# Gate and up in three PSUM banks a set, with sets that overlap by three products

## The chip, the cores and the metric

One NeuronCore of a Trainium2 chip runs the whole program. TensorE (PE) multiplies, ScalarE (ACT), VectorE (DVE) and GpSimd (POOL) work elementwise, and SyncE (SP) issues every transfer that matters here. The metric is the device time of one execution in microseconds; lower is better. Instructions of one engine run in the order of its queue, and a wait for a semaphore holds up all that stands behind it in that queue.

## The reference

The reference is one layer of a hybrid decoder block over 2064 positions (16 meta tokens and 2048 of the sequence) with 1024 channels. What matters here is its end, the SwiGLU feed-forward net with 2816 hidden channels:

```python
        h = h + mixed @ w_out[i].astype(jnp.float32)
        n2 = rmsnorm(h, norm2_g[i])
        ff = jax.nn.silu(n2 @ w_gate[i].astype(jnp.float32)) * (n2 @ w_up[i].astype(jnp.float32))
        h = h + ff @ w_down[i].astype(jnp.float32)
```

Ahead of it stand a normalisation, one projection into a state-space group and a pooling group, their normalised sum and the projection `w_out`; behind it a last normalisation. All is float32.

## The kernel before

**Arithmetic.** A float32 product is made of three fp32r matmuls (`mm3`, lines 116 to 119): each operand is split into a high part (a cast on ScalarE, line 110) and a low part (a subtraction, line 85), and the product of the two low parts is dropped. Gate, up and down use the seven products of Strassen and Winograd in place of eight. With weight quarters a11, a12, a21, a22 and their combinations s1 to s4, and activation quarters b11, b12, b21, b22 and their combinations t1 to t4, the products of one set are a11·b11, a12·b21, s2·t2, s3·t3, s1·t1, a22·t4 and s4·b22, named below by their activation (b11, b21, t2, t3, t1, t4, b22). One product is four steps of K with three matmuls of 128x512 each, so 12 matmuls into one PSUM bank. Its results are sums: c00 = b11 + b21, c01 = b11 + t2 + t1 + b22, c11 = b11 + t2 + t3 + t1, c10 = b11 + t2 + t3 + t4.

**Stages.** Until about 581 us the program does the norms, projections, the state space part, pooling and `w_out`. From 581 to 1439 us it does gate and up: for each of two halves `b` of the sequence and each of 11 steps `f0` (two blocks of 128 hidden channels) one set for gate and one for up, which is a pair of 14 products. Then it does down until the end.

**A pair.** `wset` loads the two raw weight blocks (`load_raw`, tag "raw", four buffers) and POOL makes s1, s2, s3, s4. `part` splits each of the seven into `wch` and `wcl` (ten buffers). `seven` is a generator: it gives its seven products a PSUM bank each (`mm_tile`, four banks in all). ScalarE copies the first out to a tile `u`, and VectorE does the other sums from PSUM into `u` and into the pair's tiles `gt` and `ut` (one tag, three buffers of 8 KB a partition). Gate takes Silu of its four results in place; up multiplies its four into `gt`. Then POOL makes four combinations of the four results for the down stage, and SP stores `gt` and `ut` to `ff_d` (lines 1021 and 1022). The next set begins when the one before has issued its products.

**The activations.** The seven split activation tiles `X[...]` of one half lie in SBUF, with one buffer each. `x_rows` makes them for one row block: load, norm, transposes on PE (`ptx`), copies on ScalarE, four combinations on POOL, and for all that aren't split at once a store to `xr_d`. `x_stage(b, i, n)` loads n of them for each of four row blocks (tile `xp`, tag "raw" too, so these loads, the weight loads and the row blocks `hr` share four buffers) and splits them. For the first half t2, t3 and t4 come that way, right ahead of the first pair; x_rows of the second half runs after the pairs f0 = 2, 6, 10 and 14 of the first, and its seven x_stage tiles are loaded between the halves, under a raised priority, while the last pair of the first half runs (its weights are fetched ahead: `wg`, `wu`).

**What sets the order.** The program is written once, and a scheduler assigns each instruction a place in its engine's queue, by the order of the code, priorities and an estimate of when its inputs are there. Semaphores enforce what depends on what, the reuse of buffers and banks too.

Of the kernel before, what the change touches and what calls it, by code (L numbers as in the profile page):

```python
# [9 lines left out]
F32 = mybir.dt.float32  # L10
# [3 lines left out]
AF = mybir.ActivationFunctionType  # L14
ALU = mybir.AluOpType

P = 128
# [20 lines left out]
def kernel(  # L38
# [9 lines left out]
    V, A, GP, PE, SY = nc.vector, nc.scalar, nc.gpsimd, nc.tensor, nc.sync  # L48
    M_, A_, S_ = ALU.mult, ALU.add, ALU.subtract
# [10 lines left out]
    ff_d = [dram.tile([P, NF // 2, 7, 512], F32, name=f"ff_d{b}") for b in range(NB)]  # L60
# [23 lines left out]
    def tt(o, a, b, op, e=V):  # L84
        e.tensor_tensor(o, a, b, op=op)  # L85
# [21 lines left out]
    def split(hi, lo, src, scale=None, e=V):  # L107

        if scale is None:
            A.copy(hi, src)  # L110
            tt(lo, src, hi.bitcast(F32), S_, e)
        else:
            A.activation(hi, src, AF.Copy, scale=scale)
            stt(lo, src, scale, hi.bitcast(F32), M_, S_)

    def mm3(o, lh, ll, rh, rl, first, last):
        PE.matmul(o, lh, rh, start=first, stop=False)  # L117
        PE.matmul(o, lh, rl, start=False, stop=False)  # L118
        PE.matmul(o, ll, rh, start=False, stop=last)  # L119


    ident = const.tile([P, P], F32, name="ident")
# [163 lines left out]
    for a, b in ((0, KD), (KD, nv)):  # L286
# [3 lines left out]
        if a == 0:  # L290
# [3 lines left out]
                              then=lambda: load_slice(2))  # L294
# [335 lines left out]
    done = []  # L630
# [101 lines left out]
    for u in range(NU):  # L732
        j = T + 1 + u
# [139 lines left out]
    L0, L1 = slice(0, 512), slice(512, 1024)  # L873
    HALF = T // 2

    XN = ("b11", "b21", "t2", "t3", "t1", "t4", "b22")

    def combos(b11, b12, b21, b22, put):

# [24 lines left out]
    def w_rows(m):  # L904

        ra, rb = [xa_p.tile([P, D], F32, name="wr", tag="raw", bufs=4) for _ in range(2)]
        for j, r in enumerate((ra, rb)):
            SY.dma_start(r, w_down[0][(2 * m + j) * P:(2 * m + j + 1) * P, :])
        combos(ra[:, L0], ra[:, L1], rb[:, L0], rb[:, L1], lambda nm, row: None)
        for j, r in enumerate((ra, rb)):  # L910
            SY.dma_start(wd_d[:, m, 2 * j:2 * j + 2].rearrange("p a c -> p (a c)"), r)

    def x_stage(b, i, n):

        for nm in XN[i:i + n]:
            x_tile(xb_p if nm in ("t2", "t3", "t4") else xa_p, nm)
        for t in range(HALF):
            xp = xa_p.tile([P, D], F32, name="xp", tag="raw", bufs=4)
            SY.dma_start(xp[:, :n * 512], xr_d[b][t][:, i:i + n].rearrange("p a c -> p (a c)"))
            for q in range(n):  # L920
                put_x(XN[i + q], t, xp[:, q * 512:(q + 1) * 512], GP if b and t % 2 else V)

# [14 lines left out]
    wc_p = gu.enter_context(tc.tile_pool(name="wc", bufs=1, side="right"))  # L937
    xb_p = gu.enter_context(tc.tile_pool(name="xb", bufs=1, side="right"))

    def load_raw(w, f):  # L940
        raw = xa_p.tile([P, KD, P], F32, name="raw", tag="raw", bufs=4)
        SY.dma_start(raw, w[0][:, f * P:(f + 1) * P].rearrange("(k p) f -> p k f", p=P))
# [19 lines left out]
    def seven(ws, c, done, early=False):  # L962

        a11, a12, s2, s3, s1, a22, s4 = ws

        def prod(a, xn):
            o = mm_tile("pr")
            ah, al = a if isinstance(a, tuple) else part(a)
            for k in range(4):
                mm3(o, ah[:, k], al[:, k], X[xn][0][:, k], X[xn][1][:, k], k == 0, k == 3)  # L970
            return o

        u = wc_p.tile([P, 512], F32, name="u", tag="u", bufs=2)
        A.copy(u, prod(a11, "b11"))
        yield
        tt(c(0, 0), prod(a12, "b21"), u, A_)
        done(0, 0)
        yield
        if early:
            p5, p4 = prod(s1, "t1"), prod(s4, "b22")  # L980
        tt(u, prod(s2, "t2"), u, A_)
        yield
        tt(c(1, 0), prod(s3, "t3"), u, A_)
        yield
        if not early:
            p5 = prod(s1, "t1")
        tt(c(1, 1), p5, c(1, 0), A_)
        done(1, 1)
        tt(c(0, 1), p5, u, A_)
        yield  # L990
        tt(c(1, 0), prod(a22, "t4"), c(1, 0), A_)
        done(1, 0)
        yield
        tt(c(0, 1), p4 if early else prod(s4, "b22"), c(0, 1), A_)
        done(0, 1)
        yield

    def parts(ws):
        return [part(a) for a in ws]

    def gate_up(b, f0, wg=None, wu=None):

        gt = wc_p.tile([P, 2, 2, 512], F32, name="gt", tag="gt", bufs=3)
        ut = wc_p.tile([P, 2, 2, 512], F32, name="ut", tag="gt", bufs=3)
        gate = seven(wg or wset(w_gate, f0), lambda i, j: gt[:, i, j],
                     lambda i, j: A.activation(gt[:, i, j], gt[:, i, j], AF.Silu), b == 0 and f0 == 0)  # L1006
        if wu is None:
            for _ in gate:
                pass
        next(gate, None)  # L1010
        for _ in seven(wu or wset(w_up, f0), lambda i, j: ut[:, i, j],
                       lambda i, j: tt(gt[:, i, j], gt[:, i, j], ut[:, i, j], M_)):
            next(gate, None)
        a11, a21, a12, a22 = [gt[:, i, j] for i in range(2) for j in range(2)]
        s1, s2, s4 = ut[:, 0, 0], ut[:, 0, 1], ut[:, 1, 0]
        tt(s1, a21, a22, A_, GP)
        tt(s2, s1, a11, S_, GP)
        tt(a21, a11, a21, S_, GP)
        tt(s4, a12, s2, S_, GP)
        fl = "p i j c -> p (i j) c"  # L1020
        SY.dma_start(ff_d[b][:, f0 // 2, :4], gt.rearrange(fl))
        SY.dma_start(ff_d[b][:, f0 // 2, 4:], ut.rearrange(fl)[:, :3])

    wg, wu = wset(w_gate, 0), None
    x_stage(0, 2, 2)
    x_stage(0, 5, 1)
    for b in range(NB):
        for f0 in range(0, NF, 2):
            if b == 0 and f0 == NF - 2:
                wg = parts(wset(w_gate, f0))  # L1030
                wu = wset(w_up, f0)
            gate_up(b, f0, wg, wu)
            wg = wu = None
            if b == 0 and f0 % 4 == 2 and f0 // 4 < HALF:
                x_rows(1, f0 // 4)
            if b == 1:
                w_rows(f0 // 2)
        if b == 0:
            with tc.high_priority(offset=200):
                x_stage(1, 0, 2)  # L1040
                wg = wset(w_gate, 0)
                x_stage(1, 2, 2)
                x_stage(1, 4, 2)
                x_stage(1, 6, 1)


    NM = NF // 2
# [147 lines left out]
    for g, (i, n) in enumerate(seq):  # L1195
        if g == 0:
            o, o1 = mm_tile("pd"), mm_tile("pd")
# [5 lines left out]
        elif g == 1:  # L1203
            o = o1
        else:
            o = mm_tile("pd")
# [48 lines left out]
```

## Time and profile before

| what | value |
|---|---|
| time, median of 3 runs | 1866.21 us (1865.23 to 1866.81) |
| the profiled execution's own time | 1867.75 us |
| its span, first to last instruction | 1866.0 us |
| mean granted TensorE clock | 0.987 |
| PE busy | 1803.0 us, 97% |
| DVE, POOL, ACT busy | 1240.0, 815.2, 672.6 us |

The profile is of one execution, so what is summed from it stands against 1867.75 us, and the median of the runs lies 1.5 us lower. Busy shares are of the whole span. In a timeline each row has the start in us, the duration in us, the engine, the code line, the operation with its output and inputs, and in brackets how long the engine had been idle before it and who released it; matmuls overlap in their pipeline, so the distance from start to start is the pace, not the duration. In a table of windows each row has the window, its length, for each engine the busy time and the number of instructions, then the granted clock (PEclk), the DMA engines' share and the traffic.

### The profile page before, as it was taken

How to read it: one execution, taken by the hardware profiler on the slowest of the kernel's cores; microseconds unless marked ns; L12 is line 12 of the kernel's file. 1: busy time of each engine (PE TensorE's matmuls, PEld its weight loads, DVE VectorE, ACT ScalarE, POOL GpSimd, SP SyncE). 2: the span in 40 equal slices, each digit the busy share in tenths (PEclk: the TensorE clock that was granted, in tenths of full speed). 3: DMA queues.
4: the chain of work that ended last, by engine and by line, in shares of the span. 5: the costliest groups of instructions: out<-in, count | busy, mean ns of one | idle time of the engine just before them, and what ended most of it. 6: DMA issues, size and time to landing. Idle time of an engine off the chain costs nothing.

```text
span 1866.0 us, 23676 instructions
## 1 busy us (share of the span) xinstructions
PE 1803.0 (97%) x8497; PEld 1498.3 (80%) x8497; DVE 1240.0 (66%) x1913; ACT 672.6 (36%) x1213; POOL 815.2 (44%) x619
## 2 busy tenths in 40 slices
PE   7989997899999999999999999999999999999998
PEld 5767786788877788888887788888888888888886
DVE  6995877866456877666668877777677344446773
ACT  4332334243454433333335333333333343333431
POOL 1773425733244654654646876666562000003400
PEclk9999998999999999999999999999999999999999
DMA  6254424544255353444426664455447765537871
GB/s 184 71 178 164 159 96 156 175 170 141 94 176 166 108 163 108 159 158 129 159 97 195 210 204 133 154 178 175 140 149 234 216 206 180 156 102 213 252 220 70
DMA packets 260518, 298.37 MB, mean 160 GB/s; under 512 B 17148, under 2 KB 204048, under 8 KB 255536
## 3 DMA queue, kind: packets, MB, share of 16 engines
q1 hardware_dynamic: 260304, 296.84, 50.2%
q8 instruction: 67, 1.10, 0.2%
q14 instruction: 51, 0.42, 0.1%
q0 software_dynamic: 96, 0.01, 0.0%
HBM read 202.37 MB, written 96.53 MB: 160 GB/s over the span
## 4 chain that ended last, share of the span: by engine, by line
PE 71%; DVE 3%; DMA 2%; POOL 1%; issue 1%; ACT 1%; POOLq 0%; DVEq 0%; SPq 0%; ACTq 0%
PE pr L117 13%; PE pr L119 13%; PE pr L118 13%; PE pd L118 7%; PE pd L117 7%; PE pd L119 7%; PE po L117 2%; PE po L119 2%; PE po L118 2%; DVE wcl L85 1%; POOL s L85 1%; PE pgate L774 1%; DMA hr<-h_d 1%; PE ptx L865 1%; DMA raw<-in_w_gate_dram 1%
## 5 line engine op out<-in xcount | busy, mean ns | idle before, releaser
L85 DVE TENSOR_TENSOR wcl<-raw,wch 128x512 fp32r<-128x512 f32 x176 | 179.0, 1019 | 32.1 <-ACT wch L110 31.0
L110 ACT CAST wch<-raw 128x512 fp32r<-128x512 f32 x176 | 108.7, 622 | 252.9 <-PE pr L118 226.6
L85 DVE TENSOR_TENSOR fl<-fr,fh 128x512 fp32r<-128x512 f32 x168 | 117.0, 708 | 120.6 <-ACT fh L110 120.4
L110 ACT CAST fh<-fr 128x512 fp32r<-128x512 f32 x168 | 95.7, 584 | 190.2 <-PE pd L118 165.0
L110 ACT CAST wch<-s 128x512 fp32r<-128x512 f32 x132 | 82.0, 622 | 223.8 <-PE pr L118 163.8
L85 POOL TENSOR_TENSOR s<-raw 128x512 f32<-128x512 f32 x44 | 67.3, 1531 | 167.1 <-DVE wcl L85 70.2
L85 DVE TENSOR_TENSOR wcl<-s,wch 128x512 fp32r<-128x512 f32 x132 | 121.3, 920 | 26.8 <-ACT wch L110 26.5
L85 POOL TENSOR_TENSOR db22h<-db22h,hd 128x512 f32<-128x512 f32 x4 | 5.2, 1295 | 251.9 <-DVE db22h L85 251.9
L117 PE MATMUL pj<-wh,xh 128*128 128x512 f32 x256 | 103.3, 411 | 2.3 <-ACT xh L110 2.3
L117 PE MATMUL po<-wh,mh 128*128 128x512 f32 x256 | 104.6, 409 | 0.7 <-ACT mh L110 0.7
L118 PE MATMUL pj<-wl,xh 128*128 128x512 f32 x256 | 102.9, 404 | 0.0
L119 PE MATMUL pj<-wh,xl 128*128 128x512 f32 x256 | 102.9, 406 | 0.0
L119 PE MATMUL po<-wh,ml 128*128 128x512 f32 x256 | 101.3, 397 | 0.7 <-DVE ml L85 0.7
L118 PE MATMUL po<-wl,mh 128*128 128x512 f32 x256 | 101.7, 397 | 0.0
L85 POOL TENSOR_TENSOR rs<-rv,mhalf 128x1 f32<-128x1 f32 (+2 forms) x35 | 31.4, 898 | 152.2 <-DVE rv L91 142.8
L85 DVE TENSOR_TENSOR gt<-gt,ut 128x512 f32<-128x512 f32 x88 | 96.1, 1093 | 0.0
L85 POOL TENSOR_TENSOR wr<-wr 128x512 f32<-128x512 f32 x44 | 66.7, 1516 | 67.1 <-DMA wr<-in_w_down_dram 58.6
L85 POOL TENSOR_TENSOR tmp<-z,pk 64x512 f32<-64x512 f32 x32 | 50.9, 1589 | 78.1 <-issue 64.7
L85 POOL TENSOR_TENSOR ut<-gt 128x512 f32<-128x512 f32 x22 | 34.6, 1574 | 105.8 <-DVE gt L85 105.8
L85 DVE TENSOR_TENSOR gt<-pr,gt 128x512 f32<-128x512 f32 x66 | 45.4, 689 | 51.7 <-PE pr L119 51.1
L117 PE MATMUL pr<-xt2h,wch 128*128 128x512 f32 x176 | 69.7, 396 | 6.1 <-DVE gt L85 3.6
L1006 ACT ACTIVATE gt<-gt 128x512 f32<-128x512 f32 x88 | 55.5, 632 | 52.4 <-DVE gt L85 52.4
(392 smaller groups left out, 5567.6 us busy)
## 6 DMA issues: line engine op xcount, KB each, us to landing
fr<-ff_d SPq DMA_DIRECT2D x56, 704.0 KB, 4.9
raw<-in_w_gate_dram SPq DMA_DIRECT2D x44, 512.0 KB, 4.8
raw<-in_w_up_dram SPq DMA_DIRECT2D x44, 512.0 KB, 4.6
ff_d<-gt SPq DMA_DIRECT2D x22, 1024.0 KB, 3.9
pk<-pk_d SPq DMA_DIRECT2D x16, 1284.0 KB, 6.1
ff_d<-ut SPq DMA_DIRECT2D x22, 768.0 KB, 5.6
wr<-in_w_down_dram SPq DMA_DIRECT2D x22, 512.0 KB, 3.3
wd_d<-wr SPq DMA_DIRECT2D x22, 512.0 KB, 3.5
```

What stands on the lines that cost most here:

```text
L85: e.tensor_tensor(o, a, b, op=op)
L110: A.copy(hi, src)
L117: PE.matmul(o, lh, rh, start=first, stop=False)
L118: PE.matmul(o, lh, rl, start=False, stop=False)
L119: PE.matmul(o, ll, rh, start=False, stop=last)
L774: PE.matmul(pg[:, k * P:(k + 1) * P], glubd[:, k], gt[:, k], start=True, stop=True)
L865: PE.transpose(pt[:, k], r[:, (4 * h + k) * P:(4 * h + k + 1) * P], ident)
L1006: lambda i, j: A.activation(gt[:, i, j], gt[:, i, j], AF.Silu), b == 0 and f0 == 0)
```

## The change

`seven` now uses three banks. In bank `oa` the products b11, t2, t3 and t4 are added up by TensorE itself; ScalarE copies the bank's state out after b11 (into c00), after t2 (c01) and after t3 (c11), and the next product goes on adding in the same bank once the copy is done. What is left after t4 is c10, and it goes straight from PSUM into Silu (gate) or into the multiplication (up), by the new argument `direct`. Bank `oc` takes t1 and, later, b22 on top; VectorE adds it to c11 in between and to c01 at the end. Bank `ob` takes b21, which VectorE adds to c00. The tile `u` is gone from `seven`, and its two buffers are used by the down stage's `hd` alone. The order of the products is b11, b21, t2, t1, t3, t4, b22.

Sets overlap: `run` advances a new set by its first product, then finishes the set before (`catch_up`), then advances the new one by four more steps. With the queues' own order, a steady row of products on PE is: gate b11, t3 of the up before, gate b21, gate t2, t4 and b22 of the up before, gate t1, gate t3, up b11, up b21, gate t4, gate b22, up t2, up t1, and then b11 of the next gate. The store of a pair follows its last product in `store`. The last pair of the first half keeps gate and up side by side, with `oc` in a bank of another PSUM pool (`third`), and the first set of all, marked `early`, puts its t1 and b22 ahead of t2.

The order of the activation tiles in `xr_d` changes with XN, and the first half's loads are now t2 alone (four loads of 256 KB) and then t3 with t4 (four of 512 KB), where they were t2 with t3 and then t4 alone.

```diff
-    XN = ("b11", "b21", "t2", "t3", "t1", "t4", "b22")
+    XN = ("b11", "b21", "t2", "t1", "t3", "t4", "b22")
...
+        oa = mm_tile("pr")
+        prod(oa, a11, "b11", True)
+        A.copy(c(0, 0), oa)
         yield
+        ob = mm_tile("pr")
+        prod(ob, a12, "b21", True)
+        tt(c(0, 0), ob, c(0, 0), A_)
         done(0, 0)
         yield
+        oc = third("pr")
         if early:
-            p5, p4 = prod(s1, "t1"), prod(s4, "b22")
-        tt(u, prod(s2, "t2"), u, A_)
+            prod(oc, s1, "t1", True)
+            yield
+            od = tr_tile("pr").rearrange("p k c -> p (k c)")
+            prod(od, s4, "b22", True)
+            yield
+        prod(oa, s2, "t2", False)
+        A.copy(c(0, 1), oa)
         yield
-        tt(c(1, 0), prod(s3, "t3"), u, A_)
+        if early:
+            tt(c(0, 1), oc, c(0, 1), A_)
+            tt(c(0, 1), od, c(0, 1), A_)
+            done(0, 1)
+        else:
+            prod(oc, s1, "t1", True)
+            yield
+        prod(oa, s3, "t3", False)
+        A.copy(c(1, 1), oa)
+        tt(c(1, 1), oc, c(1, 1), A_)
+        done(1, 1)
...
+        prod(oa, a22, "t4", False)
+        direct(1, 0, oa)
         yield
         if not early:
...
+            prod(oc, s4, "b22", False)
+            tt(c(0, 1), oc, c(0, 1), A_)
+            done(0, 1)
+            yield
...
+    def catch_up():
+
+        while behind:
+            gen, then = behind.pop()
+            for _ in gen:
+                pass
+            then()
+
+    def run(gen, then=lambda: None):
+
+        next(gen)
+        catch_up()
+        for _ in range(4):
+            next(gen)
+        behind.append((gen, then))
...
     wg, wu = wset(w_gate, 0), None
-    x_stage(0, 2, 2)
-    x_stage(0, 5, 1)
+    x_stage(0, 2, 1)
+    x_stage(0, 4, 2)
```

Three places of the queues show what moves. The first is SP's queue at the start of gate and up, from the loads `xp` of the first half's activations (the first two of them stand a little ahead of these rows) to the raw up weights of the first pair. Before:

```order
L817 DMA h2_d1_6_81<-hx_4973 128x1024 [waits DMAHW4_49,DVE_49]
L817 DMA h2_d1_7_82<-hx_5126 128x1024 [waits DMAHW6_49,DVE_49]
L919 DMA xp_5345<-xr_d0_2_96 128x1024 [waits DMAHW2_49,DVE_49]
L919 DMA xp_5351<-xr_d0_3_97 128x1024 [waits DMAHW3_49,DVE_49]
L919 DMA xp_5359<-xr_d0_0_94 128x512 [waits Pool_49]
L919 DMA xp_5363<-xr_d0_1_95 128x512 [waits DVE_49]
L919 DMA xp_5367<-xr_d0_2_96 128x512 [waits DMAHW6_49,DVE_49]
L919 DMA xp_5371<-xr_d0_3_97 128x512 [waits DMAHW7_49,DVE_49]
L942 DMA raw_5509<-in_w_up_dram 128x8x128 [waits DMAHW4_49,DMAHW0_49,DVE_49]
L942 DMA raw_5511<-in_w_up_dram 128x8x128 [waits DMAHW5_49,DMAHW1_49,DVE_49]
```

With the change:

```order
L1173 DMA hd_12037<-h2_d0_0_67 128x512 [waits DMASW1_49,DMASW2_49,DMASW0_49,PE_49]
L1173 DMA hd_12055<-h2_d0_1_68 128x512 [waits DMAHW6_49]
L818 DMA h2_d1_7_82<-hx_5126 128x1024 [waits DVE_49]
L920 DMA xp_5339<-xr_d0_2_96 128x512 [waits DMAHW2_49,DVE_49]
L920 DMA xp_5343<-xr_d0_3_97 128x512 [waits DMAHW3_49,DVE_49]
L920 DMA xp_5351<-xr_d0_0_94 128x1024 [waits Pool_49]
L920 DMA xp_5357<-xr_d0_1_95 128x1024 [waits DMAHW0_49,DVE_49]
L920 DMA xp_5363<-xr_d0_2_96 128x1024 [waits DMAHW4_49,DMAHW1_49,DVE_49]
L920 DMA xp_5369<-xr_d0_3_97 128x1024 [waits DMAHW5_49,DMAHW2_49,DVE_49]
L943 DMA raw_5465<-in_w_up_dram 128x8x128 [waits DMAHW6_49,DMAHW3_49,DVE_49]
L943 DMA raw_5467<-in_w_up_dram 128x8x128 [waits DMAHW7_49,DMAHW4_49,DVE_49]
```

The loads of t2 with t3 (128x1024) have become loads of t2 alone (128x512), the four loads of t4 have become loads of t3 with t4, and two loads of `hd` for the down stage have come ahead. The two loads of up weights stand behind all of them, as before. A wait for DVE here is a wait for the last split of the row block that had the buffer.

The second is POOL's queue at a pair with x_rows (f0 = 6 of the first half). `hr` are the two row blocks, `raw` the gate weights of the next pair, and `gt` and `ut` the pair that is to be stored. Before:

```order
L85 TENSOR_TENSOR ut_6288<-gt_6287 128x512 [waits DMAHW2_49,DVE_49]
L85 TENSOR_TENSOR ut_6288<-ut_6288,gt_6287 128x512 [waits Pool_49]
L85 TENSOR_TENSOR gt_6287<-gt_6287 128x512 [waits DMAHW7_49]
L85 TENSOR_TENSOR ut_6288<-gt_6287,ut_6288 128x512 [waits Pool_49]
L85 TENSOR_TENSOR hr_6581<-hr_6596,hr_6581 128x512 [waits DMAHW0_49,Activation_49]
L85 TENSOR_TENSOR hr_6596<-hr_6596 128x512 [waits Activation_49,Pool_49]
L85 TENSOR_TENSOR hr_6596<-hr_6596,hr_6581 128x512 [waits DMAHW3_49,PE_49,Pool_49]
L85 TENSOR_TENSOR hr_6581<-hr_6581,hr_6596 128x512 [waits DMAHW1_49,Pool_49]
L85 TENSOR_TENSOR s1_6922<-raw_6920 128x512 [waits DMAHW7_49,DVE_49]
L85 TENSOR_TENSOR s2_6923<-s1_6922,raw_6918 128x512 [waits Pool_49]
L85 TENSOR_TENSOR raw_6920<-raw_6918,raw_6920 128x512 [waits DVE_49]
```

With the change:

```order
L85 TENSOR_TENSOR hr_6494<-hr_6509,hr_6494 128x512 [waits DMAHW1_49,Activation_49]
L85 TENSOR_TENSOR hr_6509<-hr_6509 128x512 [waits Activation_49,Pool_49]
L85 TENSOR_TENSOR hr_6509<-hr_6509,hr_6494 128x512 [waits DMAHW3_49,PE_49,Pool_49]
L85 TENSOR_TENSOR hr_6494<-hr_6494,hr_6509 128x512 [waits DMAHW2_49,Pool_49]
L85 TENSOR_TENSOR s1_6821<-raw_6819 128x512 [waits DMAHW1_49,DVE_49]
L85 TENSOR_TENSOR ut_6215<-gt_6214 128x512 [waits DMAHW5_49,DVE_49]
L85 TENSOR_TENSOR s2_6822<-s1_6821,raw_6817 128x512 [waits DMAHW5_49,Pool_49]
L85 TENSOR_TENSOR raw_6819<-raw_6817,raw_6819 128x512 [waits DMAHW7_49,DMAHW6_49]
L85 TENSOR_TENSOR ut_6215<-ut_6215,gt_6214 128x512 [waits Pool_49]
L85 TENSOR_TENSOR gt_6214<-gt_6214 128x512
L85 TENSOR_TENSOR s4_6823<-raw_6817,s2_6822 128x512 [waits DVE_49,Pool_49]
L85 TENSOR_TENSOR ut_6215<-gt_6214,ut_6215 128x512 [waits Pool_49]
```

The four combinations of the row blocks now come first, then the next gate weights and the four operations for the store in turn, where the store's four came first of all.

The third is ScalarE's queue between the halves: the last casts of the second half's b22 (`xb22h`) and the first copies and Silu of that half's first pair. Before:

```order
L1006 ACTIVATE gt_8518<-gt_8518 128x512 [waits DVE_49]
L110 CAST xb22h_8857<-xp_8859 128x4x128 [waits DMAHW5_49,PE_49]
L110 CAST xb22h_8857<-xp_8863 128x4x128 [waits DMAHW6_49]
L110 CAST xb22h_8857<-xp_8867 128x4x128 [waits DMAHW7_49]
L110 CAST xb22h_8857<-xp_8871 128x4x128 [waits DMAHW0_49]
L974 COPY u_8877<-pr_8878 128x512 [waits PE_49]
L110 CAST wch_9022<-raw_9009 128x512 [waits DMAHW1_49,Activation_49]
L110 CAST wch_9040<-raw_9009 128x512
L1006 ACTIVATE gt_8875<-gt_8875 128x512 [waits DVE_49]
```

With the change:

```order
L110 CAST xt4h_8679<-xp_8699 128x4x128
L110 CAST xb22h_8705<-xp_8707 128x4x128 [waits DMAHW7_49,PE_49]
L110 CAST xb22h_8705<-xp_8711 128x4x128 [waits DMAHW0_49]
L110 CAST xb22h_8705<-xp_8715 128x4x128 [waits DMAHW1_49]
L994 COPY gt_8723<-pr_8725 128x512 [waits PE_49]
L110 CAST xb22h_8705<-xp_8719 128x4x128 [waits DMAHW2_49]
L110 CAST wch_8835<-raw_8823 128x512 [waits DMAHW3_49]
L110 CAST wch_8880<-raw_8823 128x512 [waits Activation_49]
L1004 COPY gt_8723<-pr_8725 128x512 [waits PE_49]
L1050 ACTIVATE gt_8723<-gt_8723 128x512 [waits DVE_49]
```

There was one copy of the set's bank behind the casts; now the copy after t2 (line 994) stands between the third and the fourth cast of b22, and the copy after t3 (line 1004) behind two casts of weights.

More of the change, by code (lines that the diff above doesn't have):

```diff
@@ L114, in split, with mm3 @@
             stt(lo, src, scale, hi.bitcast(F32), M_, S_)
[L116 to L119, printed above, removed]
+    def mm3(o, lh, ll, rh, rl, first, last, more=False):
+        PE.matmul(o, lh, rh, start=first, stop=False, skip_group_check=more)
+        PE.matmul(o, lh, rl, start=False, stop=False, skip_group_check=more)
+        PE.matmul(o, ll, rh, start=False, stop=last, skip_group_check=more)
     ident = const.tile([P, P], F32, name="ident")
@@ L960, in wset, with seven, split_of, prod @@
         return r0[:, K0], r0[:, K1], s2, r1[:, K0], s1, r1[:, K1], s4
-    def seven(ws, c, done, early=False):
+    def seven(ws, c, done, direct, early=False, third=mm_tile):
         a11, a12, s2, s3, s1, a22, s4 = ws
-        def prod(a, xn):
-            o = mm_tile("pr")
-            ah, al = a if isinstance(a, tuple) else part(a)
+        def split_of(a):
+            return a if isinstance(a, tuple) else part(a)
+        def prod(o, a, xn, first):
+            ah, al = split_of(a)
             for k in range(4):
[L970 to L974, printed above, removed]
+                mm3(o, ah[:, k], al[:, k], X[xn][0][:, k], X[xn][1][:, k], first and k == 0, k == 3, not first)
+        oa = mm_tile("pr")
+        prod(oa, a11, "b11", True)
+        A.copy(c(0, 0), oa)
@@ L975, in seven @@
         yield
-        tt(c(0, 0), prod(a12, "b21"), u, A_)
+        ob = mm_tile("pr")
+        prod(ob, a12, "b21", True)
+        tt(c(0, 0), ob, c(0, 0), A_)
         done(0, 0)
         yield
+        oc = third("pr")
         if early:
-            p5, p4 = prod(s1, "t1"), prod(s4, "b22")
-        tt(u, prod(s2, "t2"), u, A_)
-        yield
-        tt(c(1, 0), prod(s3, "t3"), u, A_)
+            prod(oc, s1, "t1", True)
[3 more added lines that the diff above has]
+            yield
@@ new lines, in seven @@
+        prod(oa, s2, "t2", False)
+        A.copy(c(0, 1), oa)
+        yield
+        if early:
[9 more added lines that the diff above has]
+        done(1, 1)
+        a22 = split_of(a22)
+        if not early:
+            s4 = split_of(s4)
+        yield
+        prod(oa, a22, "t4", False)
@@ L984, in seven @@
+        direct(1, 0, oa)
         yield
         if not early:
[L986 to L996, printed above, removed]
+            prod(oc, s4, "b22", False)
+            tt(c(0, 1), oc, c(0, 1), A_)
+            done(0, 1)
+            yield
@@ L998, in parts @@
     def parts(ws):
         return [part(a) for a in ws]
+    behind = []
+    def catch_up():
[10 more added lines that the diff above has]
+        behind.append((gen, then))
     def gate_up(b, f0, wg=None, wu=None):
@@ L1004, in gate_up, with flat, silu, times @@
         ut = wc_p.tile([P, 2, 2, 512], F32, name="ut", tag="gt", bufs=3)
+        def flat(nm):
+            return tr_tile(nm).rearrange("p k c -> p (k c)")
+        def silu(i, j, src):
+            A.activation(gt[:, i, j], src, AF.Silu)
+        def times(i, j, src):
+            tt(gt[:, i, j], gt[:, i, j], src, M_)
+        def store():
+            a11, a21, a12, a22 = [gt[:, i, j] for i in range(2) for j in range(2)]
+            s1, s2, s4 = ut[:, 0, 0], ut[:, 0, 1], ut[:, 1, 0]
+            tt(s1, a21, a22, A_, GP)
+            tt(s2, s1, a11, S_, GP)
+            tt(a21, a11, a21, S_, GP)
+            tt(s4, a12, s2, S_, GP)
+            fl = "p i j c -> p (i j) c"
+            SY.dma_start(ff_d[b][:, f0 // 2, :4], gt.rearrange(fl))
+            SY.dma_start(ff_d[b][:, f0 // 2, 4:], ut.rearrange(fl)[:, :3])
@@ L1005, in gate_up @@
+        third = mm_tile if wu is None else flat
         gate = seven(wg or wset(w_gate, f0), lambda i, j: gt[:, i, j],
-                     lambda i, j: A.activation(gt[:, i, j], gt[:, i, j], AF.Silu), b == 0 and f0 == 0)
+                     lambda i, j: silu(i, j, gt[:, i, j]), silu, b == 0 and f0 == 0, third)
         if wu is None:
[L1008 to L1022, printed above, removed]
+            run(gate)
+        else:
+            next(gate)
+            catch_up()
@@ L1024 @@
+        up = seven(wu or wset(w_up, f0), lambda i, j: ut[:, i, j],
+                   lambda i, j: times(i, j, ut[:, i, j]), times, False, third)
+        if wu is None:
+            run(up, store)
+        else:
+            for _ in up:
+                next(gate, None)
+            store()
     wg, wu = wset(w_gate, 0), None
-    x_stage(0, 2, 2)
-    x_stage(0, 5, 1)
+    x_stage(0, 2, 1)
+    x_stage(0, 4, 2)
     for b in range(NB):
@@ L1044 @@
                 x_stage(1, 6, 1)
+    catch_up()
     NM = NF // 2
```

## The prediction

> **What bounds the kernel now.** I read the page's busy times first, then its chain, then a table of 50 us windows over gate and up, then TensorE's waits in the two windows that are not full.
>
> ```profile
> PE 1803.0 (97%) x8497; PEld 1498.3 (80%) x8497; DVE 1240.0 (66%) x1913; ACT 672.6 (36%) x1213; POOL 815.2 (44%) x619
> PE 71%; DVE 3%; DMA 2%; POOL 1%; issue 1%; ACT 1%; POOLq 0%; DVEq 0%; SPq 0%; ACTq 0%
> 600.00:650.00 50.00, 48.19 (x212) 39.31 (x211) 40.13 (x50) 18.03 (x33) 28.46 (x19) 1.00 0.45 135
> 750.00:800.00 50.00, 50.00 (x222) 41.44 (x221) 32.13 (x44) 15.91 (x27) 25.99 (x18) 1.00 0.53 171
> 1000.00:1050.00 50.00, 45.87 (x193) 36.95 (x192) 39.90 (x43) 22.51 (x40) 37.26 (x26) 0.97 0.67 216
> 1350.00:1400.00 50.00, 50.00 (x222) 41.43 (x221) 36.19 (x44) 15.14 (x25) 32.32 (x22) 1.00 0.45 143
> ```
>
> The chain is TensorE's. In a steady window it is busy for 50.00 of 50 us, while VectorE, whose work the change cuts, is busy for 32 to 36. 222 matmuls in 50 us are 0.225 us each, so a product of 12 takes 2.70 us and a pair of 14 takes 37.8. Nothing that VectorE is spared can shorten a steady pair. Time can be gained only where TensorE waits:
>
> ```profile
> PE pr L117 <- DVE ut L85: 1.8, 2, 1.1
> PE pr L117 <- ACT xt2h L110: 1.4, 1, 1.4
> PE pr L117 <- ACT wch L110: 0.7, 1, 0.7
> PE pr L119 <- DVE wcl L85: 0.4, 1, 0.4
> PE pr L117 <- DVE gt L85: 4.1, 3, 2.0
> PE pr L117 <- DVE u L85: 0.7, 1, 0.7
> 1020.00:1023.00 3.00, 1.46 (x4) 0.77 0.79 228
> 1023.00:1026.00 3.00, 3.00 (x11) 0.66 0.76 229
> ```
>
> The first four rows are the window 560 to 700 us (the start of gate and up), the next two 960 to 1100 (between the halves); the last two are 3 us windows of TensorE, with the granted clock ahead of the last two numbers. The waits are 4.3 and 4.8 us. After one of them, of 2.0 us, the clock fell, which cost 1.46 x 0.23 + 3.00 x 0.34 = 1.4 us. So the most there is to gain is 4.3 + 4.8 + 1.4 = 10.5 us, 0.6%.
>
> **The change part by part.** *Steady pairs.* TensorE does the same 3696 matmuls (22 pairs x 14 x 12) at the same pace; adding to a bank is what 11 of the 12 matmuls of a product do already. Per pair eight of VectorE's sums from PSUM go and four ScalarE copies come:
>
> ```profile
> L85 DVE TENSOR_TENSOR gt<-pr,gt 128x512 f32<-128x512 f32 x66 | 45.4, 689 | 51.7 <-PE pr L119 51.1
> L974 ACT COPY u<-pr 128x512 f32<-128x512 f32 x44 | 25.5, 580 | 1.4 <-PE pr L119 1.4
> ```
>
> That is 176 x 0.69 = 121 us less for VectorE and 88 x 0.58 = 51 us more for ScalarE, both off the path. The new wait is of TensorE for a copy before the bank is added to again. Between two products of a bank there is at least one other product, 2.70 us, and a copy of 0.58 with one cast as long ahead of it takes 1.2. I take nothing for it. Without that cover it would be 0.6 to 1.2 us six times a pair, 80 to 158 us in all.
>
> A second new wait: ScalarE now copies into `ut` right after the set's first product, and that buffer is the one of the `gt` before, so the copy waits for the pair's store to land. TensorE needs that copy before up's t2, six products (16.2 us) after the pair's last matmul, E.
>
> ```profile
> 1210.84 0.39 PE L119 MATMUL pr<-xb22h,wcl 128*128 128x512 f32 x1
> L1021 SPq DMA_DIRECT2D ff_d<-gt x1: 338/338/338, 1219.8 to 1219.8; - x1
> DMA to landing us min/median/max: 4.2/4.2/4.2
> ```
>
> Here E is 1211.2 and the store is issued 8.6 later and lands after 4.2: E + 12.8, copied at E + 13.4. That is 2.8 us early, so a steady pair costs nothing. ScalarE stands still meanwhile, but the casts behind are for the next set, more than a product away.
>
> *Pairs with x_rows (four).* POOL now makes the row blocks' combinations, then the next gate's s1, and only then and in turn the store's operations. TensorE's transposes push up's t2 to E + 19.6 (7 products are 18.9, the rest is what the walk of the new queue leaves of other work).
>
> ```profile
> 750.25 6.59 POOL L85 TENSOR_TENSOR hr<-hr 128x512 f32<-128x512 f32 x4
> 759.73 1.30 POOL L85 TENSOR_TENSOR s<-raw 128x512 f32<-128x512 f32 x1 [2.90 <-DMA raw<-in_w_gate_dram]
> ff_d<-gt SPq DMA_DIRECT2D x22, 1024.0 KB, 3.9
> raw<-in_w_gate_dram SPq DMA_DIRECT2D x44, 512.0 KB, 4.8
> xr_d<-hr SPq DMA_DIRECT2D x40, 256.0 KB, 4.2
> ```
>
> The row blocks' copies are there about E - 7.6. Two combinations of 1.65 and a store that must land bring the third to E - 1.3. Its result is stored (4.2) before that buffer takes the gate weights (4.8): s1 can start about E + 8. Then come s1 and five operations before the store of `gt`, 1.3 to 1.7 each as in the rows, 8.4 in all: E + 16.3. The store lands in 3.9, the copy takes 0.6: E + 20.8 against 19.6, a stall of 1.2 to 1.5 us. The first such pair is less regular. I take three of 1.3, +4 us; the bounds are 0 (transfers 1.5 us faster) and +11 (load and store each 1.3 us slower, four times).
>
> *The start.* The first two columns of a timeline's rows are start and duration.
>
> ```profile
> 581.30:604.20 22.90, 21.07 (x87) 15.91 (x88) 2.46 (x4) 0.58 (x1) 1.00 0.65 184
> 587.48 9.27 SPq L919 DMA_DIRECT2D xp<-xr_d  x6
> 592.73 0.63 ACT L1006 ACTIVATE gt<-gt 128x512 f32<-128x512 f32 x1
> 593.17 0.39 PE L119 MATMUL pr<-xb22h,wcl 128*128 128x512 f32 x1
> 593.90 0.69 DVE L85 TENSOR_TENSOR xt2l<-xp,xt2h 128x512 fp32r<-128x512 f32 x1 [1.15 <-ACT xt2h L110]
> 594.96 0.50 PE L117 MATMUL pr<-xt2h,wch 128*128 128x512 f32 x1 [1.40 <-ACT xt2h L110]
> 597.03 1.01 SPq L942 DMA_DIRECT2D raw<-in_w_up_dram  x2
> 601.32 1.14 ACT L110 CAST wch<-raw 128x512 fp32r<-128x512 f32 x2 [1.13 <-DMA raw<-in_w_up_dram]
> xp<-xr_d SPq DMA_DIRECT2D x16, 512.0 KB, 4.6
> ```
>
> The first four products end at 593.6 in both. Before, t2 starts at 595.0, t2, t3 and t4 follow, and up's first product begins at about 603.7 on weights that were loaded at 597.0 and cast at 601.3. With the change t2 alone is there some 1.4 us sooner and runs from 593.6 to about 597. Then TensorE's next product is up's b11, and t3 stands behind it. The up weights are at the end of SP's queue, and their buffer is that of the second load of t3 and t4. That load in turn waits for the split of t2's third row block, about 593.5. So: 593.6, + 4.6 to land, + 0.6 for two casts and 1.3 for the last of two splits, is 600.1 minus some overlap, say 599.8; + 4.3 as the up load took (601.3 less 597.0), + 0.5 for a cast: TensorE goes on at about 604.5. It has waited some 7.5 us where it waited 1.4. At 604.2 before had 87 matmuls done, now 60: 27 x 0.225 = 6.1 us behind.
>
> Such an idle time cost clock elsewhere in this trace:
>
> ```profile
> 96.00:99.00 3.00, 1.04 (x5) 0.60 0.72 246
> 99.00:102.00 3.00, 3.00 (x9) 0.50 0.24 54
> 102.00:105.00 3.00, 3.00 (x14) 0.76 0.68 226
> ```
>
> TensorE had stood still from 93 to about 98, and lost 1.04 x 0.40 + 3 x 0.50 + 3 x 0.24 = 2.6 us. I take 1.4, the cost after 2.0 us of idle time (above), the smaller of two rows. Against it, VectorE's late sums at 624 to 633 (`DVE ut`, 1.8 us) go, since VectorE has 10 such operations a pair in place of 18. The start is then +6.1 + 1.4 - 1.8 = +5.7, between +1 (t3's loads overlap, no clock lost) and +10.
>
> The Trainium skill ("TensorE: Matmul & The Clock Gate", "What's actually happening") has the clock halve after at least one idle window of about 3.4 us, and return after about as long of busy time. By that rule the start would lose 3.4 x 0.5 = 1.7 us, and the sum be 0.3 higher; but the wait of 2.0 us between the halves would have cost nothing, and the rows at 1020 show 0.77 and 0.66. The trace decides: shorter idle times count too.
>
> *Between the halves.* The `DVE gt` waits (4.1) are of a bank that VectorE had not read in time. With fewer sums most of them and the clock loss should go, 6.2 us with the `u` wait. But a bank is added to again sooner after the activations arrive. On ScalarE the copy after t2 stands behind three casts of b22, which before came in from 1022 to 1025:
>
> ```profile
> 1023.91 0.62 ACT L110 CAST xb22h<-xp 128x512 fp32r<-128x512 f32 x1 [0.81 <-DMA xp<-xr_d]
> 1028.07 1.14 ACT L110 CAST wch<-raw 128x512 fp32r<-128x512 f32 x2 [2.19 <-DMA raw<-in_w_up_dram]
> ```
>
> TensorE would have started that half at 1013, so its third product ends at 1021, and the copy is done at about 1025.1, 1.4 us after t1 has ended at 1023.7. With the clock still to pay that is 2.5 us. Up's b11 is due two products earlier than before, about 1027, and its weights are cast at 1028.7: 0.6 of it remains after the first wait. So 3.1 are left of 6.2, -3 us; bounds -6 and +3 (both waits double).
>
> *The end.* The last pair's products come earlier or later by at most two products against down's first; the stored results were due 3 us before they are read in my walk. Zero, at worst +3.
>
> The sum: 0 + 4 + 5.7 - 3 = +6.7 on the profiled execution's 1867.75 us, 1874.5. The median of the runs is 1.5 lower, which gives 1873.
>
> **The rivals.** *VectorE's relief wins.* All waits at both places go: if SP's loads land earlier than I reckon, t3 and the up weights arrive by 597. For it: nearly all waits are named after VectorE. Against it: the up weights' place in SP's queue. Half of 10.5 to all of it: 1856 to 1861.
>
> *It cancels.* Start and middle come out even and the stores of the x_rows pairs land in time: +5.7 - 6 = about 0, so 1863 to 1869. For it: the x_rows stall is 1.2 us, what is left between two sums of eight durations and more.
>
> *The store comes too late in every pair.* From a store that lands later than E + 15.6 on, each of some 20 pairs that follow another stalls; my margin is 2.8 us. For it: the second store of a pair, of `ut`, is slower and shares the queue:
>
> ```profile
> ff_d<-ut SPq DMA_DIRECT2D x22, 768.0 KB, 5.6
> ```
>
> Against it: the buffer that is waited for is that of `gt`. At 1 us too late it is +20 on the forecast, 1893.
>
> *It does not do what it says*: the copies don't run between the products but in TensorE's way, behind casts that come late. If the 88 added ones cost their 0.58 us each, that is +51, 1917. I give it little, since another product of 2.70 us stands between.
>
> **How the numbers follow.** My forecast, slower by 3 to 14 us through the start and the x_rows pairs, has a chance of 0.55; even 0.20; VectorE's relief 0.18; the late store 0.05; copies in the way 0.02. A measurement of this kernel can tell 0.2% (3.7 us) from no change, so faster means below 1862.5 and slower above 1869.9. Of the forecast nearly all lies above that; slower is 0.60, the same 0.22, faster 0.18. The likeliest case's own range is 1869 to 1880. The range for 8 in 10 reaches into the relief case, where a gain of 5 us is 1861, and leaves out its lower end and the late store: 1861 to 1881.
>
> **What would show it.** Right: one idle time of 5 to 9 us on TensorE at 597 to 605, ended by the cast of up weights or by their load, with a clock below 1.00 after it; in three or four pairs near 700 to 950 a wait of TensorE for a ScalarE copy into `ut`; windows of 50.00 of 50 elsewhere; VectorE's busy time near 1120. Wrong: no such idle time at the start, waits for copies in steady pairs from 1100 on, or a steady window with fewer than 222 matmuls.

## The result: 1% slower

The changed kernel takes 1885.95 us in the median (1884.30 to 1888.42, four runs) against 1866.51 for the kernel before (four runs): a ratio of 1.0105, 95% interval 1.0087 to 1.0122. The forecast of 1873 had the sign, but not the size; the time lies above its range. The changed kernel's profiled execution took 1885.13 us, its span is 1883.4 and so 17.4 longer.

The page of the changed kernel, its busy times and the chain:

```profile
PE 1806.2 (96%) x8497; PEld 1496.8 (79%) x8497; DVE 1124.2 (60%) x1738; ACT 711.3 (38%) x1301; POOL 806.6 (43%) x619
PE 69%; DMA 3%; DVE 3%; POOL 2%; issue 2%; ACT 1%; DVEq 0%; POOLq 0%; SPq 0%; ACTq 0%
```

VectorE has 116 us less to do (1240.0 before), ScalarE 39 more. The chain is still TensorE's. TensorE's waits over gate and up (560 to 1480 us), and four 50 us windows:

```profile
PE pr L118 <- ACT wch L110: 8.6, 3, 6.8
PE pr L118 <- ACT ut L979: 5.8, 2, 5.2
PE pr L118 <- ACT gt L994: 4.0, 1, 4.0
PE pr L118 <- DVE ut L85: 1.1, 1, 1.1
PE pr L118 <- DVE gt L85: 1.0, 1, 1.0
PE pr L119 <- DVE xt2l L85: 0.3, 1, 0.3
```

```profile
600.00:650.00 50.00, 46.40 (x192) 36.98 (x192) 37.49 (x40) 20.77 (x38) 29.24 (x20) 0.94 0.44 139
750.00:800.00 50.00, 49.36 (x218) 40.55 (x217) 27.37 (x35) 17.67 (x31) 22.34 (x17) 1.00 0.44 137
1050.00:1100.00 50.00, 42.66 (x172) 33.66 (x171) 33.00 (x33) 16.27 (x29) 36.37 (x26) 0.93 0.60 191
1350.00:1400.00 50.00, 50.00 (x222) 41.39 (x222) 27.38 (x31) 17.40 (x30) 34.66 (x24) 1.00 0.44 149
```

The waits on VectorE have gone from 7.0 us to 2.4, as they were meant to. In their place stand waits on ScalarE: for a cast of weights (`wch`), for the copy into `ut` (line 979) and for the copy after t2 (line 994). A steady window (1350 to 1400) is as full as before, 222 matmuls in 50 us, and VectorE is busy for 27 us in it instead of 36. The loss lies elsewhere.

Both traces hold all 3696 matmuls of gate and up, so the start of the n-th can be compared. The table has how far the changed kernel lags behind the kernel before, in us, and what each stretch adds. A stretch adds what the change's own waits and lost clock cost there, less what the waits of the kernel before cost.

| stretch of gate and up | lag at its end | added |
|---|---|---|
| first matmul | -1.07 | |
| start: to the 240th | 6.05 | +7.1 |
| pairs with x_rows: to the 1836th | 7.33 | +1.3 |
| between the halves: to the 2040th | 8.81 | +1.5 |
| second pair of the second half: to the 2200th | 17.03 | +8.2 |
| to the 3544th | 17.03 | 0.0 |
| end of the program | 17.4 | +0.3 |

The last large step in TensorE's timeline, and its windows behind it:

```profile
1091.94 0.79 PE L118 MATMUL pr<-xt2h,wch 128*128 128x512 f32 x1 [5.19 <-ACT ut L979]
```

```profile
1091.00:1094.00 3.00, 2.06 (x5) 0.51 0.20 82
1094.00:1097.00 3.00, 3.00 (x9) 0.50 0.55 175
1097.00:1100.00 3.00, 3.00 (x13) 0.85 0.00 0
```

The wait of 5.2 us is followed by 2.06 x 0.49 + 3 x 0.50 + 3 x 0.15 = 3.0 us of lost clock: 8.2 together. Why the copy is late there is told by the timeline's rows of the copy, of the store that it waits for, and of VectorE and POOL ahead of that store; the second view is of the tile `gt` from 1080 to 1092 us, with the time from that store's issue to its landing:

```profile
1076.20 0.68 DVE L85 TENSOR_TENSOR ut<-pr,ut 128x512 f32<-128x512 f32 x1
1077.90 1.77 DVE L85 TENSOR_TENSOR gt<-gt,ut 128x512 f32<-128x512 f32 x1
1079.75 1.67 POOL L85 TENSOR_TENSOR ut<-gt 128x512 f32<-128x512 f32 x1 [0.63 <-DVE gt L85]
1083.08 1.74 POOL L85 TENSOR_TENSOR gt<-gt 128x512 f32<-128x512 f32 x1
1082.11 1.01 SPq L943 DMA_DIRECT2D raw<-in_w_up_dram  x2
1084.84 0.47 SPq L1063 DMA_DIRECT2D ff_d<-gt  x1
1091.31 0.59 ACT L979 COPY ut<-pr 128x512 f32<-128x512 f32 x1 [9.51 <-DMA ff_d<-gt]
```

```profile
DMA to landing us min/median/max: 6.4/6.4/6.4
```

The pair's last matmul, E, ended at 1073.2. The store of `gt` is issued at E + 11.6, behind a last sum that VectorE makes only at E + 3.0 and a multiplication that ends at E + 6.5. It lands after 6.4 us, with three loads of raw weights issued in the 5.3 us before it (1079.6 to 1083.1). The copy is done at 1091.9, and TensorE had been free since 1086.8, which is E + 13.6.

### The profile page after: what moved, and what is told of

Same layout as the page of the kernel before. It is cut to its first block, busy times and chain, and to the rows that moved or that the text cites. A ratio compares the mean times of both kernels' runs of the same rounds, so it can differ in the third digit from the quotient of the medians.

```text
span 1883.4 us, 23464 instructions
## 1 busy us (share of the span) xinstructions
PE 1806.2 (96%) x8497; PEld 1496.8 (79%) x8497; DVE 1124.2 (60%) x1738; ACT 711.3 (38%) x1301; POOL 806.6 (43%) x619
## 4 chain that ended last, share of the span: by engine, by line
PE 69%; DMA 3%; DVE 3%; POOL 2%; issue 2%; ACT 1%; DVEq 0%; POOLq 0%; SPq 0%; ACTq 0%
PE pr L118 13%; PE pr L119 12%; PE pr L120 12%; PE pd L119 7%; PE pd L118 7%; PE pd L120 7%; PE po L118 2%; PE po L120 2%; PE po L119 2%; DVE wcl L85 1%; DMA xp<-xr_d 1%; DMA hr<-h_d 1%; PE pgate L775 1%; PE ptx L866 1%; DMA ff_d<-gt 1%
## 5 line engine op out<-in xcount | busy, mean ns | idle before, releaser
L85 DVE TENSOR_TENSOR wcl<-raw,wch 128x512 fp32r<-128x512 f32 x176 | 191.8, 1099 | 139.6 <-ACT wch L110 139.6
L85 DVE TENSOR_TENSOR wcl<-s,wch 128x512 fp32r<-128x512 f32 x132 | 115.7, 880 | 80.8 <-ACT wch L110 80.7
L85 DVE TENSOR_TENSOR ut<-pr,ut 128x512 f32<-128x512 f32 x66 | 45.3, 686 | 68.6 <-ACT ut L979 39.0
L118 PE MATMUL pr<-xb11h,wch 128*128 128x512 f32 x176 | 69.8, 397 | 8.6 <-ACT wch L110 8.6
L118 PE MATMUL pr<-xt3h,wch 128*128 128x512 f32 x176 | 69.4, 394 | 4.0 <-ACT gt L994 4.0
```

Source lines behind the costliest of these rows:

```text
L118: PE.matmul(o, lh, rh, start=first, stop=False, skip_group_check=more)
```

## The experiments

Each run's ratio is to the kernel before, taken on the same chip; the changed kernel has 1.0105. Where the stretches of the table are used, they are counted from the first matmul of gate and up: the part of the program ahead of it, whose code no run changes, began gate and up between 7.9 us earlier and 2.2 later than in the trace of the kernel before, from one execution to the next.

| run | ratio (95%) | start | x_rows | middle | store | end |
|---|---|---|---|---|---|---|
| the change | 1.0105 (1.0087 to 1.0122) | 7.1 | 1.3 | 1.5 | 8.2 | 0.3 |
| old loads | 1.0100 (1.0086 to 1.0114) | 6.7 | 1.8 | 2.2 | 6.4 | 0.5 |
| old loads, gate first | 1.0083 (1.0069 to 1.0097) | 1.1 | 1.2 | 1.8 | 8.6 | 1.3 |
| gate first alone | 1.0082 (1.0065 to 1.0098) | 4.7 | 2.5 | 1.9 | 6.4 | 1.5 |
| own tile for c00 | 1.0045 (1.0032 to 1.0059) | 5.3 | 0.0 | 2.4 | 1.1 | 0.3 |
| casts on VectorE | 1.0093 (1.0079 to 1.0107) | 6.9 | 2.1 | 4.0 | 7.0 | 0.3 |
| up weights ahead of b22 | 1.0073 (1.0054 to 1.0092) | 6.6 | 1.6 | -1.2 | 5.4 | 2.6 |
| down weights later | 1.0065 (1.0048 to 1.0082) | 7.0 | 1.7 | -0.4 | 0.0 | 4.2 |
| three repairs | 1.0017 (1.0006 to 1.0028) | 2.4 | -0.5 | 0.6 | 1.9 | 1.1 |
| four repairs | 1.0054 (1.0037 to 1.0071) | 0.9 | -0.5 | 1.8 | 0.0 | 5.9 |
| five repairs | 1.0049 (1.0030 to 1.0067) | 0.9 | -0.5 | 2.3 | 0.0 | 5.4 |

The columns are us added in one profiled execution's trace, at the places of the table above, with all that follows the 2200th matmul under "end"; the ratio is of all timed runs. One trace stands behind each row, and a place that an edit leaves alone still differs from one row to another: the start lies between 5.3 and 7.1, the store between 6.4 and 8.6. So a difference below 2 us in one column is not read as an effect. By time alone, the own tile, the later down weights and the three runs with several repairs are clear of the change's interval; the other five overlap it, and what is said of them rests on their traces.

**The start: the loads, the order, or both.** The first run takes the loads of the kernel before for the first half (and their order in `xr_d`), and nothing else:

```diff
-    x_stage(0, 2, 1)
-    x_stage(0, 4, 2)
+    x_stage(0, 2, 2)
+    x_stage(0, 5, 1)
```

> The changed kernel (1885.95 us), but the first half's activations are loaded as in the kernel before: t2 with t3 in four loads, then t4 alone; order of the products and overlap of the sets as changed. Theory L (the split of the loads makes the 6.8 us wait at the start): t3 is there with t2, the raw up weights are loaded about as early as before, and the start costs nothing: about 7 us less, 1879. Theory O (the order of TensorE's queue makes it: up's b11 stands ahead of t3, and its weights come last whatever the loads): a wait of 3 to 5 us for the cast of up's weights stays at 598 to 602, and the time falls by 2 to 3, to 1883.

The second also finishes the first pair's gate set before up begins:

```diff
             run(gate)
+            if b == 0 and f0 == 0:
+                catch_up()
```

> As the run before, and in the first pair of all the gate set is finished before up begins, so that t3 and t4 stand ahead of up's b11 as in the kernel before. Theories L and O both expect the start to cost what it did before: no wait over 2 us between 592 and 606, and 7 us less than the changed kernel, 1879. If it is less than 4 us better, neither the loads nor the order explains the start.

The third has this order with the change's own loads:

> The changed kernel with its own loads at the start (t2, then t3 with t4), but the first pair's gate set is finished before up begins, so t3 stands ahead of up's b11. In the traces the start (from the first product to the 240th matmul) cost 7.1 us with the change, 6.7 with the old loads alone, and 0.7 to 1.1 with the old loads and this order. Theory O (the order of TensorE's queue alone): the start costs at most 2 us, ratio to the kernel before about 1.0075. Theory L+O (both are needed: t3's loads come one by one after t2's, so t3 too is late): t3 is split at about 601, a wait of 4 to 5 us stays, ended by t3 and not by up's weights, and the ratio is 1.0095 or more.

TensorE's waits from 585 to 640 us in the three, in this order, the longest of each:

```profile
PE pr L118 <- ACT wch L110: 4.7, 1, 4.7
```

```profile
PE pr L118 <- ACT xt2h L110: 1.4, 1, 1.4
```

```profile
PE pr L118 <- ACT xt3h L110: 2.9, 1, 2.9
```

With the old loads alone, the wait for up's weights is 4.7 us, as theory O had it, but the start is only 0.4 us cheaper: t2, which the change had brought forward by 1.8 us, is late again. With the old loads and the old order the start costs 1.1, and the longest wait left is t2's 1.4, which the kernel before has too. With the old order alone the wait is for t3 and the start costs 4.7. That lies between the two theories of this run, which had at most 2 us of start, or a wait of 4 to 5. So both are needed: the loads alone give 0.4 of 7.1, the order alone 2.4, both 6.0. The second run's own figure, 7 us of time, was missed by its ratio (1.0083, 4 us less), and its trace says why: the start gave back 6.0, but the store's wait, at 8.6, and the end, 0.9 us worse, did not move with it.

**The wait for the store.** Up's c00 gets a tile of its own, so that the first write to the pair's buffer is the copy after t2:

```diff
+        u00 = wc_p.tile([P, 512], F32, name="u", tag="u", bufs=2)
+
+        def uc(i, j):
+            return ut[:, i, j] if i or j else u00
```

> The changed kernel, but up's c00 has a tile of its own (two buffers of 2 KB, which the changed kernel left to the down stage), so that up's first write to the pair's tile comes after t2 and not after b11. Theory S (the copy after up's b11 waits for the store of an older tile to land, and TensorE's t2 waits for the copy): the wait of 5.2 us near 1087 and the 0.6 at 774 go, with the clock lost after them: 8 to 9 us less than the changed kernel, 1877. Rival (the wait is only the last in a row, since VectorE, GpSimd and the transfers are late there anyway): the wait moves to the copy after t2 or to another tile, and the time falls by less than 3 us, above 1883.

The x_rows waits are gone (0.0), and of the store's 8.2 us 1.1 is left, in a wait of 0.8 at the copy after t2. TensorE's waits from 960 to 1120 us:

```profile
PE pr L118 <- ACT wch L110: 7.2, 1, 7.2
PE pr L118 <- ACT ut L994: 0.8, 1, 0.8
```

The store itself was no sooner: it was issued at E + 20.4. That is theory S: 8.4 us of trace in these two stretches, and 0.6% of time (1.0045 against 1.0105, 11 us). Between the halves a single wait of 7.2 us for a cast of up's weights takes the place of several, at a like sum (2.4 against 1.5).

Whether the crowd after the halves meet makes that store late was asked by a run that begins the down weights' combinations two pairs later:

```diff
-            if b == 1:
-                w_rows(f0 // 2)
+            if b == 1 and f0 >= 4:
+                w_rows(f0 // 2 - 2)
+                if f0 >= NF - 4:
+                    w_rows(f0 // 2)
```

> The changed kernel, but the down weights' combinations begin two pairs later in the second half (two are made after each of the last two pairs), so that GpSimd and the transfers have less to do after the halves meet. The store of the pair at 1085 was issued 11.8 us after its last matmul, where a steady pair takes some 8.6, and landed after 6.4 us and not 3.9. Theory D (the crowd of work after the halves meet makes this one store late): the wait of 5.2 us becomes less than 1, 8 us less, ratio 1.006. Rival N (the margin is too short there whatever runs beside it, since up's t2 comes 13.6 and not 16.2 us after the last matmul): a wait of 2 us or more stays, ratio 1.008 or more.

The store of the same pair and ScalarE's copy in the timeline, and the store's landing:

```profile
1083.98 0.34 SPq L1063 DMA_DIRECT2D ff_d<-gt  x1
1087.93 0.59 ACT L979 COPY ut<-pr 128x512 f32<-128x512 f32 x1 [1.66 <-DMA ff_d<-gt]
```

```profile
DMA to landing us min/median/max: 3.9/3.9/3.9
```

The wait is 0. E is at 1077.6 there, so the store is issued at E + 6.4 and lands after 3.9. The gain is theory D's 8.2 us in that stretch, but 2.6 us of waits for the store came back in the last two pairs, where two combinations are made instead of one. The run can't separate the crowd from the margin in full, since the scheduler now also put up's t2 behind gate's t4 and b22. That order alone doesn't do it: the run with up's weights ahead of b22 (below) has it too, and keeps a wait of 3.4 us at that place. And the copy was done at E + 10.9, which would have been in time for the change's own t2 at E + 13.6 as well.

**Between the halves.** The four casts of the second half's b22 go to VectorE (`dve` is true for them alone), so the copy after t2 no longer stands behind them:

```diff
-            A.copy(hi, src)
+            (V.tensor_copy if dve else A.copy)(hi, src)
```

> The changed kernel, but the four casts of the second half's b22 run on VectorE, so that ScalarE's copy after t2 of that half's first gate set no longer stands behind them. Theory C (the copy's place behind the casts makes the 4.0 us wait at 1031.5): the wait and the clock lost after it go, about 5 to 6 us less than the changed kernel, 1880. Rival T (the transfers between the halves set it: the raw up weights were cast at 1038.0 only): a wait of about 4 us comes two products later, for the cast of up's weights, and the time stays within 1.5 us, 1884.5 to 1886.

The waits from 960 to 1120 us:

```profile
PE pr L118 <- ACT wch L110: 5.8, 2, 4.1
PE pr L118 <- ACT ut L979: 4.6, 1, 4.6
```

The copy's wait is gone, and one of 4.1 us for the cast of up's weights stands in its place: rival T. The middle is not better (4.0 against 1.5), nor is the time clear of the change's. The next run loads those weights ahead of b22:

```diff
                 x_stage(1, 4, 2)
+                wu = wset(w_up, 0)
                 x_stage(1, 6, 1)
```

> The changed kernel, but between the halves the first raw up weights are loaded ahead of the second half's b22. The run with the casts on VectorE showed that the wait only passes from the copy to the up weights. Theory T (the transfers set it): the up weights are cast about 5 us sooner, at 1033, the waits of 4.0 and 1.1 shrink to about 2 in sum, and the stretch from the 1836th to the 2040th matmul, which cost 1.5 us more than before, costs 3 to 4 less; ratio 1.008 if the store's wait near 1087 stays. Rival: b22 is late in its turn and nothing is gained, ratio 1.0105.

```profile
PE pr L118 <- ACT ut L979: 3.4, 1, 3.4
PE pr L118 <- ACT wch L110: 2.2, 1, 2.2
PE pr L118 <- ACT xt1h L110: 0.6, 1, 0.6
PE pr L118 <- ACT ut L1004: 0.5, 1, 0.5
```

The wait for weights is 2.2 us, none for the copy after t2 is left, and the stretch costs 2.7 us less than with the change, where theory T expected 3 to 4. So the order of the transfers bears on the middle; but in the runs below that have this repair too the stretch costs 0.6 to 2.3, so the gain did not carry over whole.

**All together.** Three repairs in one kernel: old loads with gate first in the first pair, the tile for c00, and up's weights ahead of b22.

> The changed kernel with the three repairs at once: old loads and gate finished first in the first pair, a tile of its own for up's c00, and the up weights ahead of b22 between the halves. If the three places are all that the change lost, then in the trace the start costs 1 us, the x_rows pairs 0, the middle -2 to +2 and the store's wait 0, against the kernel before: a ratio of 0.9985 to 1.002. If it stays above 1.004 some cost of the change lies elsewhere.

The ratio is 1.0017 (1.0006 to 1.0028), as expected if these places are all that the change lost. The trace adds 5.5 us: 2.4, -0.5, 0.6, 1.9 and 1.1; the start and the store were expected at 1 and 0. Two more runs added the later down weights, and then the casts on VectorE:

> The run with the three repairs, and the down weights' combinations begun two pairs later in the second half. With the three repairs 1.6 us of a wait for the store was left (1.9 us with what went with it), now at the copy after t2. Theory D (the crowd after the halves meet makes that store late): it goes, and the stretch from the 2040th to the 2200th matmul costs 0; but the two late combinations cost some 2 us near the end, as they did alone. Ratio to the kernel before 1.000 to 1.002. A version faster than the kernel before would need the end to stay as it is: ratio 0.999. Rival: above 1.003, the late combinations cost more at the end than the store's wait.

> As the run before, and the casts of the second half's b22 on VectorE. Alone this moved a wait of 4.0 us from ScalarE's copy to the up weights, which are now loaded earlier. If the two bound the middle together, the waits left between the halves (2.9 and 1.5 us with three repairs) shrink below 2 in sum and the stretch from the 1836th to the 2040th matmul costs 2 to 3 us less than with three repairs: ratio 0.998 to 1.001. Rival: the transfers set the middle in any case and nothing is gained: same ratio as the run before.

Both are worse than with three, 1.0054 and 1.0049. The store's stretch is 0.0 in both, but the end costs 5.9 and 5.4. These runs were expected at 1.000 to 1.002 and 0.998 to 1.001; the rival of the first, above 1.003 through the end, came. From 1120 us on TensorE has this wait in the run with four repairs, of down's first matmul for its first results:

```profile
PE pd L118 <- ACT fh L110: 3.9, 1, 3.9
```

Counted from the first matmul of gate and up, the load of these results lands 2.7 us later than with three repairs, behind a store of the pair that is issued 8 us later; the stores of the late combinations stand ahead of both. That fits the late combinations as the cause, but no run takes them apart from the rest. The casts on VectorE took nothing from the middle either (2.3 against 1.8), so the rival held for both runs. No version was faster than the kernel before.

## Why the prediction was right and wrong

**The bound.** Right: steady windows hold 222 matmuls with the change too, and VectorE's 116 us bought nothing there. The new wait for a copy before a bank is added to again costs nothing in a steady pair: from 1130 to 1430 us no wait of TensorE is named at all. There ScalarE does wait for stores, 23.5 us in eight waits, and TensorE for none of it, as the margin of 2.8 us said.

**The start.** Predicted +5.7, measured +7.1. The mechanism held: t2 sooner, then a long wait for up's weights behind t3's loads, 6.8 us where I had 7.5. The clock lost behind it cost more than my 1.4:

```profile
602.54 0.80 PE L118 MATMUL pr<-xb11h,wch 128*128 128x512 f32 x1 [6.82 <-ACT wch L110]
```

```profile
600.00:603.00 3.00, 0.46 (x1) 0.50 0.89 257
603.00:606.00 3.00, 3.00 (x8) 0.50 0.76 207
606.00:609.00 3.00, 3.00 (x13) 0.94 0.62 176
```

It is 0.46 x 0.50 + 3 x 0.50 + 3 x 0.06 = 1.9 us, between my two rows, 1.4 and 2.6. That is not the difference, since the wait was 0.7 shorter: up to the 73rd matmul the lag grew by 7.3, where I had 7.5. The 1.4 over my sum came behind it. The lag grew by 1.8 more up to the 133rd, with a wait of 1.0 for VectorE to read a bank (`DVE gt`), a term that I had at nothing; then VectorE's late sums gave back 1.9, where I had 1.8.

```profile
619.70 0.50 PE L118 MATMUL pr<-xt1h,wch 128*128 128x512 f32 x1 [0.96 <-DVE gt L85]
```

**Pairs with x_rows.** Predicted +4 from three stalls of 1.3; measured +1.3, from one named wait of 0.6 and smaller losses. The place and the copy it waits for were right, the size three times too large. The term that was off is the chain ahead of s1, which I had done at E + 8: in the last three of these pairs s1 started at E + 7.3, 6.2 and 5.7. The store of `gt` then went out at E + 15.8, 15.2 and 14.7 and not 16.3, so the copy was done at E + 20.3, 19.6 and 19.2 against a t2 due at E + 19.7. Only the first of the three is late, by that 0.6; in the pair before them, the first with x_rows, the store went out at E + 12.5. With the tile for c00 the stretch costs 0.0, and -0.5 in the three other runs that have it, against 1.2 to 2.5 in all that don't, which shows that the copy's wait for the store was the cause.

**Between the halves.** Predicted -3, measured +1.5. The step that failed is "So 3.1 are left of 6.2": the new waits cost 9.0 us, against 7.5 that the old ones gave back. The waits on VectorE went as predicted (the lag falls from 7.3 to 2.7, and by 2.9 more further on). The copy's wait behind b22's casts came, but with its clock it was 5.9 us (4.0 of wait) and not 2.5:

```profile
1033.70 1.27 ACT L110 CAST xb22h<-xp 128x512 fp32r<-128x512 f32 x2 [1.20 <-DMA xp<-xr_d]
1034.87 0.58 ACT L994 COPY gt<-pr 128x512 f32<-128x512 f32 x1
1035.50 0.50 PE L118 MATMUL pr<-xt3h,wch 128*128 128x512 f32 x1 [3.98 <-ACT gt L994]
```

The wait for up's weights took 1.5 (1.1 of wait) and not 0.6, and one of 1.1 for a bank, 1.7 with what followed, was not in my sum. What the runs point to in its place: the loads of this half set the middle, and TensorE waits at whichever point first needs the last of them, since moving a cast or a load moved the wait. The DMA engines were not full, 0.53 busy from 1020 to 1030 us; the first load of b22 was issued at 1029.2, against 1019.2 before and a lag of 7.3. What held these loads back stays open.

**The store.** This is the step that cost the forecast its range: "so a steady pair costs nothing" was carried over to all pairs without x_rows, and the second pair of the second half is not steady. All three terms of the sum were worse there. I had the store issued at E + 8.6; it was E + 11.6. I had it land after 4.2; it took 6.4. I had up's t2 due at E + 16.2; the queue has it after five products and not six, at E + 13.6. My margin of 2.8 less 3.0, 2.2 and 2.6 is -5.0, and the wait was 5.2. The rival "the store comes too late in every pair" had this mechanism, with a chance of 0.05; it came in one pair, at the price of 8.2 us. Without this stretch the change would have added 9.2 us, 2.5 from my sum of 6.7.

**The rivals.** VectorE's relief did win at its own waits, and lost what it won to transfers and their casts. Nothing cancelled. That the copies stand in TensorE's way all along is excluded by the steady windows.

**The clock.** The Trainium skill ("TensorE: Matmul & The Clock Gate", "What's actually happening") lets the clock halve after at least one idle window of about 3.4 us and return after at least one busy window of about that length. The wait of 6.8 us agrees with one: 0.46 + 3.0 us and a little at 0.50. The wait of 5.2 took longer: 2.06 + 3.0 + 0.9 us, some 6.0 at about half. By the rule the clock would have cost the start 1.7 us; it cost 1.9.

## What to carry to other kernels

Where TensorE is full, as in these steady windows, work taken from another engine is worth only the waits it causes, and a new order of products has to be paid at the seams: the first set, the change from one half to the next, and the pairs next to it. A margin found in a steady stretch should be worked out again at each seam with the queue of that place, since the due time, the issue and the landing all shift there together. A buffer that is written earlier in a set makes the store of its last user part of the path; a small tile for the first result took that off.

## What the runs showed of the hardware

A wait of TensorE cost more than its length: 6.8 us became 9.0 (the lag from the 49th to the 73rd matmul), 5.2 became 8.2 and 4.0 became 5.9 (the lag from 2.7 to 8.5), since the granted clock stood near 0.5 for 3.5 to 6 us after it. A store of 1 MB landed after 6.4 us when three weight loads were issued in the 5.3 us before it, and after 5.7 to 6.9 in the five other runs with three such loads ahead of the same store; it landed after 3.9 in the run with later down weights, where one load was issued in that time, 5.0 us before it. The same code ahead of gate and up ended between 573.5 and 583.6 us from one profiled execution to another, so stretches of a trace had to be compared from a common point.
